# Stick-breaking attention block on one core: the later modulation moved behind attention, the convolution off GpSimd, more split weights in stock

## The chip, the cores and the metric

The kernel runs on one core of one Trainium2 chip. The metric is the device time of one execution in microseconds (us); a kernel's time is the median of its runs. In the profile PE is TensorE's matmuls, PEld its weight loads, DVE is VectorE, ACT is ScalarE, POOL is GpSimd and SP is SyncE, whose queue issues most loads. "Lnnn" is a line of the kernel file.

## The reference

One layer (DEPTH = 1) on a sequence of 1024 tokens of width 1024, all in float32:

```python
mod = c_act @ ada_w[l] + ada_b[l]                  # c_act = silu(c)
sh1, sc1, g1, sh2, sc2, g2 = split(mod, 6)         # sections 0 to 5
h = rmsnorm(x, ln1_g[l]) * (1.0 + sc1) + sh1
p = h @ w_in[l]                                    # 1024 x 8192
q, k, v, cb, cc, cx, ga, gb = split(p)             # eight times 1024
q, k = rmsnorm of q and k per head (16 heads of 64)
y_a = stick_breaking_attention(q, k, v)
y_b = cb * causal_dwconv(cc * cx, conv_w[l])       # three taps per channel
merged = sigmoid(ga) * (y_a @ w_branch_a[l]) + sigmoid(gb) * (y_b @ w_branch_b[l])
x = x + g1 * (merged @ w_out[l])
h = rmsnorm(x, ln2_g[l]) * (1.0 + sc2) + sh2
f = (silu(h @ w_ffn_gate[l]) * (h @ w_ffn_up[l])) @ w_ffn_down[l]
x = x + g2 * f
```

For a query t and a key s < t, stick-breaking attention weighs v[s] by sigmoid(z[t,s]) times the product of 1 - sigmoid(z[t,j]) over the keys j between s and t, with z = q.k / 8.

## The kernel before, in words

Every large product is made of three fast matmuls: each operand is split into a high and a low part in a rounded 32-bit format (`whi` and `wlo` for a weight), and high x high, high x low and low x high are added up in PSUM. A split is a copy on ACT (the high part) and a subtraction on DVE (the low part). So a weight that has been loaded can be used by PE only after ACT and then DVE have had it.

The work goes through these stages:

- **Start** (to about 60 us): the norm of x, and sections 0 and 1 of the modulation.
- **Keys and half of the values** (to about 190 us).
- **Gate stage** (about 190 to 620 us): the loop over `gates` makes, in this order, the queries (section 5 of the list, four steps), the two inputs of the convolution (sections 1 and 2 alternating, eight steps) and the two sigmoid gates (sections 4 and 3, eight steps). Each step is a product of a 1024 x 256 block of weights with all of h by Strassen's scheme: seven products (`g_prod`) of twelve matmuls instead of eight. Its sums of weights (`ws`) are made on POOL; weights and sums are split by `g_split`, whose buffers `whi` and `wlo` are `GS` = 4 deep. The results are put together on DVE (`c`). `put_q` squares a query tile on POOL and splits the square for the sums that the norm needs (L540). `put_u` multiplies the two inputs of the convolution on POOL and makes the three taps: one on POOL, one on ACT, a sum on POOL, the last one on DVE.
- In the gate stage runs also the generator `mods_later`: it makes the later sections 2 to 5 of the modulation. For each section eight tiles of 128 x 1024 (`mada`, two buffers) are loaded from ACT's queue and summed into `macc` with the entries of c as factors (L492, L494 on DVE); then small matmuls with ones sum over the partitions (L253 for columns, L507 for the rows that are broadcast). Three steps of it are taken per gate step from the fifth on. Sections 2 and 5 (g1 and g2) go to DRAM (`d_g`), sections 3 and 4 stay in `mod`.
- **Attention** (about 625 to 1080 us): per head and block of 128 queries scores on PE, two sigmoids on ACT, a scan (L710) and a product (L712) on DVE, transposes, a split and the product with v. Between them, as fillers, run the other values, the product of `cb` with the convolution, whose split result (`ybh`, `ybl`, the low part on POOL, L829) goes to DRAM and comes back, and the branch-b product.
- **Branch-a product** (about 1090 to 1185 us): the loop `for m in range(KT)` loads a weight (`load_ch`), makes two groups of 24 matmuls in two PSUM banks, multiplies with the gate, adds branch b (L933, L934) and splits. `preload_wo` loads and splits the first three output weights in a pool `wpx` that lies where the attention's pool was.
- **Output product with the second norm** (to about 1275 us), **gate and up of the FFN** (to about 1700 us), **down** (to the end).

Tiles are allocated in pools that are opened and closed like a stack on two sides of SBUF; a tile in a new pool waits for those that lay there before. The order of instructions on each engine is not the program's: a scheduler places them by a simulated timeline, with the program's order as priority, and the chip then keeps to that order in each engine's queue. DMAs are issued from the queues of SP, ACT and POOL, in order with what else stands there.

Of the kernel before, what the change touches and what calls it, by code (L numbers as in the profile page):

```python
# [8 lines left out]
F32 = mybir.dt.float32  # L9
F32R = mybir.dt.float32r  # L10
AF = mybir.ActivationFunctionType
# [18 lines left out]
def block_kernel(tc, x, x_t, cols, ada_1, ada_2, ada_row, w_q, w_kv, w_v1, w_cg, w_a, w_b, w_o, w_g, w_u, w_d, out):  # L30
# [8 lines left out]
    def nm(s):  # L39
        uid[0] += 1  # L40
        return f"{s}_{uid[0]}"
# [54 lines left out]
    cst = const.tile([P, 82], F32, name="cst")  # L96
    nc.scalar.dma_start(cst, cols)
    ct, ln1, ln2 = cst[:, 0:8], cst[:, 8:16], cst[:, 16:24]
    acol = cst[:, 24:56].rearrange("p (m k) -> p m k", m=4)
    cw = cst[:, 56:80].rearrange("p (k t) -> p k t", k=8)  # L100
    qgc, kgc = cst[:, 80:81], cst[:, 81:82]
    nc.vector.tensor_scalar(out=qgc, in0=qgc, scalar1=0.125, scalar2=None, op0=ALU.mult)
    mod = const.tile([P, 4, 8], F32, name="mod")
    rqs = ExitStack()
# [144 lines left out]
    def mod_cols(m, acc, k0, kn):  # L249

        ps = g_ss()
        for j in range(kn):
            nc.tensor.matmul(ps[:, j:j + 1], acc[:, j * P:(j + 1) * P], ones[:, 0:1], start=True, stop=True)  # L253
        nc.vector.tensor_tensor(out=mod[:, m, k0:k0 + kn], in0=ps[:, :kn], in1=acol[:, m, k0:k0 + kn], op=ALU.add)

    def norm_x(k, n):
        src = xt[:, k, n * 512:(n + 1) * 512]
# [174 lines left out]

    last_raw = [None]

    def g_split(src):
        hi = gw.tile([P, 512], F32R, tag="whi", bufs=GS, name=nm("whi"))
        lo = gw.tile([P, 512], F32R, tag="wlo", bufs=GS, name=nm("wlo"))
        nc.scalar.activation(hi, src, AF.Copy)  # L438
        tt(nc.vector, lo, src, hi.bitcast(F32), ALU.subtract)
        return hi, lo  # L440
# [35 lines left out]
    gp = sg_.enter_context(tc.tile_pool(name="phg1", bufs=1, reuse_waits="tile"))  # L476

    ft[6] = gp.tile([P, 2, 4, 512], F32R, name="ft6")
    for q, t in ft.items():
        fac[q] = (t[:, 0], t[:, 1])  # L480
    fac[3] = (hh[1][:, 0:4], hl[1][:, 0:4])

    def mods_later():

        for sec in SECS:
            acc = gp.tile([P, D], F32, tag="macc", bufs=1, name=nm("macc"))
            for k in range(8):
                ad = gp.tile([P, D], F32, tag="mada", bufs=2, name=nm("mada"))
                with tc.issue_after(evac[0].ins):
                    nc.scalar.dma_start(ad, ada_2[SECS.index(sec), k])  # L490
                if k == 0:
                    nc.vector.tensor_scalar(out=acc, in0=ad, scalar1=ca[:, k:k + 1], scalar2=None, op0=ALU.mult)  # L492
                else:
                    nc.vector.scalar_tensor_tensor(out=acc, in0=ad, scalar=ca[:, k:k + 1], in1=acc,  # L494
                                                   op0=ALU.mult, op1=ALU.add)
                yield
            yield
            yield
            if sec in (3, 4):
                mod_cols(sec - 1, acc, 0, 8)  # L500
            else:
                e = 0 if sec == 2 else 1
                gb_ = gp.tile([P, D], F32, tag="mada", bufs=2, name=nm("mgb"))
                nc.scalar.dma_start(gb_, ada_row[e:e + 1, :].broadcast_to([P, D]))
                for n in range(2):
                    ps = g_ss()
                    nc.tensor.matmul(ps, ones, acc[:, n * 512:(n + 1) * 512], start=True, stop=True)  # L507
                    nc.vector.tensor_tensor(out=gb_[:, n * 512:(n + 1) * 512], in0=ps,
                                            in1=gb_[:, n * 512:(n + 1) * 512], op=ALU.add)
                nc.scalar.dma_start(d_g[e], gb_)  # L510
            yield

    def g_ss():
        return ps_tr()

    ssq = [g_ss()[:H] for n in range(2)]
    evac = [None]
    ml = mods_later()
# [9 lines left out]
    def put_q(c, m, n):  # L528

        sq = g_tile()  # L530
        tt(nc.gpsimd, sq, c, c, ALU.mult)
        sh, sl, hi, lo = (g_tile(F32R) for _ in range(4))
        nc.scalar.activation(hi, c, AF.Identity, scale=qgc)
        nc.vector.scalar_tensor_tensor(out=lo, in0=c, scalar=qgc, in1=hi.bitcast(F32), op0=ALU.mult, op1=ALU.subtract)
        for e, t in ((0, hi), (1, lo)):
            nc.scalar.dma_start(d_q[e][m, :, n * 512:(n + 1) * 512], t.bitcast(F32))
        nc.scalar.activation(sh, sq, AF.Copy)
        tt(nc.vector, sl, sq, sh.bitcast(F32), ALU.subtract)
        for t in (sh, sl):
            nc.tensor.matmul(ssq[n], sel[:, 14 - 2 * m:30 - 2 * m], t, start=(nss[n] == 0), stop=(nss[n] == 15))  # L540
            nss[n] += 1
# [18 lines left out]
    def put_u(c, m, n):  # L560

        u = uu[m // 4]
        s = n * 512
        tt(nc.gpsimd, u[:, 2 + s:514 + s], c, ccs[m, n], ALU.mult)
        if n == 0:
            uc[m] = True
        elif not uc.get(m):
            raise ValueError(m)
        y, y1 = g_tile(), g_tile()
        nc.gpsimd.tensor_scalar(out=y, in0=u[:, s + 2:s + 514], scalar1=cw[:, m, 2:3], scalar2=None, op0=ALU.mult)  # L570
        nc.scalar.activation(y1, u[:, s + 1:s + 513], AF.Copy, scale=cw[:, m, 1:2])
        tt(nc.gpsimd, y, y, y1, ALU.add)
        nc.vector.scalar_tensor_tensor(out=y, in0=u[:, s:s + 512], scalar=cw[:, m, 0:1], in1=y, op0=ALU.mult, op1=ALU.add)
        nc.scalar.dma_start(d_y[m, :, s:s + 512], y)

# [6 lines left out]
    for g, (sec, j) in enumerate(gates):  # L582
# [31 lines left out]
                with tc.issue_after(ws4.ins):  # L614
                    next(eq, None)

        evac[0] = nc.scalar.activation(c11, p1, AF.Copy)
# [21 lines left out]
        if g + 1 == len(gates):  # L639
            for _ in eq:  # L640
                pass
        for _ in range((0 if sec == 5 else 3) if g + 1 < len(gates) else 50):
            next(ml, None)
    sg_.close()
    gws.close()
    ftx.close()
    gws = ExitStack()
    gw = gws.enter_context(tc.tile_pool(name="wpb", bufs=1, side="right", reuse_waits="tile"))
    for e in range(2):
        nc.sync.dma_start((hh, hl)[e][1][:, :4].bitcast(F32), d_h[e])  # L650
    psA.close()
# [137 lines left out]
    def fillers():  # L789
# [24 lines left out]
        for m, n in [(m, n) for m in range(KT - 2) for n in range(2)] + [(m, n) for n in range(2) for m in (KT - 2, KT - 1)]:  # L814
            if n == 0:
                cb_w[m] = load_ch(w_cg[0, m])
            w = cb_w[m]
            y = fp.tile([P, 512], F32, tag="st", bufs=3, name=nm("cy"))
            nc.sync.dma_start(y, d_y[m, :, n * 512:(n + 1) * 512])
            ps = ps_f()  # L820
            for kk in range(0, KT, KQ):
                if kk:
                    yield 0.65 * KQ
                mm_ch(ps, w, hh[n], hl[n], kk, kk + KQ)
            nc.vector.tensor_tensor(out=y, in0=ps, in1=y, op=ALU.mult)
            yh = fq.tile([P, 512], F32R, tag="ybh", bufs=2, name=nm("ybh"))
            yl = fq.tile([P, 512], F32R, tag="ybl", bufs=2, name=nm("ybl"))
            nc.scalar.activation(yh, y, AF.Copy)  # L828
            nc.gpsimd.tensor_tensor(out=yl, in0=y, in1=yh.bitcast(F32), op=ALU.subtract)  # L829
            nc.scalar.dma_start(d_yb[0][n][:, m, :], yh.bitcast(F32))  # L830
            nc.scalar.dma_start(d_yb[1][n][:, m, :], yl.bitcast(F32))
            yield 0.65 * KQ
# [54 lines left out]
    fqpool.close()  # L887


    swx = ExitStack()  # L890
    wx = swx.enter_context(tc.tile_pool(name="wpx", bufs=1, side="right", reuse_waits="tile"))
    w_pre = []

    def preload_wo():
# [469 lines left out]
```

## Time and profile before

| | |
|---|---|
| median of 3 runs | 1940.23 us (1938.12 to 1941.57) |
| profiled execution | 1936.22 us |
| its span | 1934.4 us |
| granted TensorE clock, mean | 0.986 |
| busy PE / DVE / ACT / POOL | 1850.6 / 1462.6 / 865.2 / 637.7 us |
| moved by DMA | 347.47 MB, mean 180 GB/s |

A row of the instruction groups reads: line, engine, operation, output<-input with shapes, count | busy time in us, mean of one in ns | idle time of the engine before them and who ended it. Matmuls overlap and their ends are modelled, so the distance from start to start tells the pace of PE, and a "busy" PE need not be at its peak. A row of the waits reads: who waited, for whom, us in total, times, longest.

### The profile page before, as it was taken

Reading aid. Unit: us, or ns where it says so; the run is one execution under the profiler, and the core shown is the slowest. Engines: PE = TensorE matmul, PEld = TensorE weight load, DVE = VectorE, ACT = ScalarE, POOL = GpSimd, SP = SyncE. Lnnn points to the kernel's source line nnn. Section 1 sums busy time; section 2 is a strip of 40 time slices with the busy share of each in tenths; the row PEclk is TensorE's granted clock in tenths of the full one; section 3 lists DMA queues with packets and bytes.
Section 4 is the critical chain, followed back from the end, with each engine's and each line's share of the span. In section 5 each row is a group of like instructions: output and inputs, shape, how many; then the busy total and the mean of one; then the engine's idle time right before and its main releaser. Section 6 shows DMA issues by size and latency. Waiting matters only on the chain.

```text
span 1934.4 us, 25157 instructions
## 1 busy us (share of the span) xinstructions
PE 1850.6 (96%) x8869; PEld 1518.1 (78%) x8869; DVE 1462.6 (76%) x1960; ACT 865.2 (45%) x1597; POOL 637.7 (33%) x453
## 2 busy tenths in 40 slices
PE   7899999998999899999999999979999999999999
PEld 4678767777888888887888788867888888888787
DVE  8865787788664799998999644389988788843855
ACT  4532343223333677776777421373444434422221
POOL 3693647977231001111000000055445445301013
PEclk8999999999999999999999999999999999999999
DMA  6555544334445666668654535423444434389666
GB/s 277 178 189 173 201 158 158 131 114 159 161 171 201 207 168 182 169 175 286 178 161 132 190 124 190 139 87 115 158 158 169 153 140 164 133 310 336 246 222 224
DMA packets 151149, 347.47 MB, mean 180 GB/s; under 512 B 15088, under 2 KB 52208, under 8 KB 149104
## 3 DMA queue, kind: packets, MB, share of 16 engines
q1 hardware_dynamic: 74000, 218.80, 34.3%
q10 hardware_dynamic: 76016, 123.40, 17.7%
q0 software_dynamic: 1008, 3.67, 0.5%
q8 instruction: 70, 1.15, 0.2%
q14 instruction: 55, 0.45, 0.1%
HBM read 235.19 MB, written 110.62 MB: 179 GB/s over the span
## 4 chain that ended last, share of the span: by engine, by line
PE 44%; DVE 10%; DMA 3%; issue 2%; ACT 2%; POOL 0%; SPq 0%; ACTq 0%; DVEq 0%
PE e L122 6%; PE e L123 6%; PE e L124 6%; PE e L1203 3%; PE e L1204 3%; PE e L1202 3%; PE pj L785 3%; PE pj L786 3%; PE pj L787 3%; DVE pt L710 2%; PE tr L726 1%; DVE wlo L965 1%; PE e L1020 1%; PE e L1022 1%; PE e L1021 1%
## 5 line engine op out<-in xcount | busy, mean ns | idle before, releaser
L710 DVE TENSOR_TENSOR_SCAN pt<-pt,dm 128x256 f32<-128x256 f32 (+7 forms) x128 | 174.0, 1363 | 4.7 <-ACT pt L705 4.6
L123 PE MATMUL e<-big,whi 128*128 128x512 f32 x352 | 138.4, 393 | 7.6 <-DVE big L127 7.5
L122 PE MATMUL e<-big,whi 128*128 128x512 f32 x352 | 138.0, 392 | 0.8 <-ACT c L1118 0.8
L124 PE MATMUL e<-big,wlo 128*128 128x512 f32 x352 | 137.9, 392 | 0.0
L124 PE MATMUL pj<-big,wlo 128*128 128x512 f32 x320 | 127.5, 399 | 6.6 <-DVE wlo L127 6.6
L276 PE MATMUL pj<-whi,big 128*128 128x512 f32 x352 | 116.8, 412 | 15.0 <-ACT big L263 10.3
L122 PE MATMUL pj<-big,whi 128*128 128x512 f32 x320 | 128.1, 400 | 0.2 <-ACT whi L438 0.2
L1203 PE MATMUL e<-wlo,f 128*128 128x512 f32 (+1 forms) x319 | 122.9, 385 | 4.7 <-DVE wlo L965 4.7
L123 PE MATMUL pj<-big,whi 128*128 128x512 f32 x320 | 127.1, 397 | 0.0
L705 ACT ACTIVATE pt<-z,rq 128x512 f32<-128x512 f32 (+2 forms) x192 | 112.5, 588 | 30.4 <-PE z L704 17.3
L1204 PE MATMUL e<-whi,f 128*128 128x512 f32 (+1 forms) x319 | 122.2, 384 | 0.0
L113 POOL TENSOR_SCALAR rs_m<-ss 128x1 f32<-128x1 f32 x8 | 1.5, 192 | 361.9 <-ACT xn L1035 361.9
L127 DVE TENSOR_TENSOR c<-e,c 128x512 f32<-128x512 f32 x154 | 102.9, 682 | 21.0 <-PE e L124 21.0
L1202 PE MATMUL e<-whi,f 128*128 128x512 f32 (+1 forms) x319 | 117.2, 385 | 1.2 <-DVE c L127 1.2
L829 POOL TENSOR_TENSOR ybl<-cy,ybh 128x512 fp32r<-128x512 f32 x16 | 29.0, 1812 | 257.6 <-ACT ybh L828 243.4
L438 ACT ACTIVATE whi<-raw 128x512 fp32r<-128x512 f32 x116 | 72.7, 633 | 91.9 <-PE pj L123 33.5
L706 ACT ACTIVATE sg<-z,rq 128x512 f32<-128x512 f32 (+1 forms) x192 | 112.9, 591 | 1.3 <-DVE mb L851 1.3
L127 DVE TENSOR_TENSOR wlo<-ws,whi 128x512 fp32r<-128x512 f32 x80 | 73.8, 942 | 50.9 <-ACT whi L438 50.9
L127 DVE TENSOR_TENSOR c<-pj,c 128x512 f32<-128x512 f32 x140 | 93.2, 682 | 24.1 <-PE pj L124 24.0
L730 DVE TENSOR_TENSOR atl<-tr,ath 128x512 fp32r<-128x512 f32 (+1 forms) x192 | 100.5, 545 | 9.8 <-ACT ath L729 9.4
L729 ACT ACTIVATE ath<-tr 128x512 fp32r<-128x512 f32 (+1 forms) x192 | 90.4, 498 | 35.8 <-PE tr L726 15.3
L127 POOL TENSOR_TENSOR ws<-raw,raw 128x512 f32<-128x512 f32 x41 | 57.3, 1398 | 144.5 <-DMA raw<-w_cg 96.0
(250 smaller groups left out, 5602.9 us busy)
## 6 DMA issues: line engine op xcount, KB each, us to landing
f<-d_f SPq DMA_DIRECT2D x77, 512.0 KB, 4.3
d_f<-fs ACTq DMA_DIRECT2D x70, 512.0 KB, 2.6
raw<-w_cg SPq DMA_DIRECT2D x40, 512.0 KB, 3.4
mada<-ada ACTq DMA_DIRECT2D x32, 512.0 KB, 4.2
raw<-w_g SPq DMA_DIRECT2D x24, 512.0 KB, 3.2
raw<-w_u SPq DMA_DIRECT2D x23, 512.0 KB, 3.2
d_k<-khl ACTq DMA_DIRECT2D x32, 256.0 KB, 2.2
d_q<-gt ACTq DMA_DIRECT2D x32, 256.0 KB, 2.0
```

Source lines behind the costliest of these rows:

```text
L122: nc.tensor.matmul(ps, wh[:, k, :], fh[:, k, :], start=(k == 0), stop=False)
L123: nc.tensor.matmul(ps, wh[:, k, :], fl[:, k, :], start=False, stop=False)
L124: nc.tensor.matmul(ps, wl[:, k, :], fh[:, k, :], start=False, stop=(k == 3))
L127: eng.tensor_tensor(out=out, in0=a, in1=b, op=op)
L276: nc.tensor.matmul(ps, a, b, start=(k == 0 and q == 0), stop=(k == KT - 1 and q == 2))
L705: nc.scalar.activation(pt[:, off + s0:off + s0 + m], z[:, :m], AF.Sigmoid, scale=rq[:, 1, i, h:h + 1])
L706: nc.scalar.activation(sg[:, s0:s0 + m], z[:, :m], AF.Sigmoid, scale=rq[:, 0, i, h:h + 1])
L710: nc.vector.tensor_tensor_scan(out=pt[:, rev], data0=pt[:, rev], data1=dm[:, rev], initial=0.0, op0=ALU.mult, op1=ALU.add)
L730: nc.vector.tensor_tensor(out=tl[:, :nb, c0:c0 + P], in0=src, in1=th[:, :nb, c0:c0 + P].bitcast(F32), op=ALU.subtract)
L1202: nc.tensor.matmul(o, sh, w[0][:, c], start=(j == 0), stop=False)
L1203: nc.tensor.matmul(o, sh, w[1][:, c], start=False, stop=False)
L1204: nc.tensor.matmul(o, sl, w[0][:, c], start=False, stop=(j == NJ - 1))
```

## The change

It has three parts.

- The later modulation leaves the gate stage. The generator is rebuilt and runs in the branch-a loop, six steps in each of the first six rounds, the rest in the seventh. c is broadcast to all partitions (`cab`) and multiplied with its sigmoid. The weights lie transposed in DRAM, so that one instruction, `tensor_tensor_reduce`, multiplies a tile of 128 x 1024 with `cab` and sums along the row into one column of `ms`. Sections 3 and 4 add their bias and are done. Sections 2 and 5 add theirs and are broadcast by eight small matmuls with the identity each. The tiles `mada` have five buffers, in a new pool `wpm`; `wpx` opens when it is closed. Bias rows for sections 2 and 5 come with the constants, so two broadcast loads of them go.
- In `put_q` the square goes from POOL to ACT. In `put_u` the product u goes from POOL to DVE, the first tap from POOL to ACT, and the second tap and the sum become one multiply-add on DVE. In the fillers `ybl` goes from POOL to DVE.
- `g_split` takes its buffers in turn from two pools, in the gate stage from `gw` and `gp`, so that eight split weights can stand ready.

```diff
+    gcol = cst[:, 82:98].rearrange("p (m k) -> p m k", m=2)
...
+    split_at = [gw]
+
     def g_split(src):
-        hi = gw.tile([P, 512], F32R, tag="whi", bufs=GS, name=nm("whi"))
-        lo = gw.tile([P, 512], F32R, tag="wlo", bufs=GS, name=nm("wlo"))
+        split_at.append(split_at.pop(0))
+        hi = split_at[0].tile([P, 512], F32R, tag="whi", bufs=GS, name=nm("whi"))
+        lo = split_at[0].tile([P, 512], F32R, tag="wlo", bufs=GS, name=nm("wlo"))
...
+    split_at.append(gp)
...
-    def mods_later():
-
-        for sec in SECS:
-            acc = gp.tile([P, D], F32, tag="macc", bufs=1, name=nm("macc"))
-            for k in range(8):
-                ad = gp.tile([P, D], F32, tag="mada", bufs=2, name=nm("mada"))
-                with tc.issue_after(evac[0].ins):
-                    nc.scalar.dma_start(ad, ada_2[SECS.index(sec), k])
-                if k == 0:
-                    nc.vector.tensor_scalar(out=acc, in0=ad, scalar1=ca[:, k:k + 1], scalar2=None, op0=ALU.mult)
-                else:
-                    nc.vector.scalar_tensor_tensor(out=acc, in0=ad, scalar=ca[:, k:k + 1], in1=acc,
-                                                   op0=ALU.mult, op1=ALU.add)
-                yield
...
     def put_q(c, m, n):
 
         sq = g_tile()
-        tt(nc.gpsimd, sq, c, c, ALU.mult)
+        nc.scalar.activation(sq, c, AF.Square)
...
-        tt(nc.gpsimd, u[:, 2 + s:514 + s], c, ccs[m, n], ALU.mult)
+        tt(nc.vector, u[:, 2 + s:514 + s], c, ccs[m, n], ALU.mult)
...
-        y, y1 = g_tile(), g_tile()
-        nc.gpsimd.tensor_scalar(out=y, in0=u[:, s + 2:s + 514], scalar1=cw[:, m, 2:3], scalar2=None, op0=ALU.mult)
-        nc.scalar.activation(y1, u[:, s + 1:s + 513], AF.Copy, scale=cw[:, m, 1:2])
-        tt(nc.gpsimd, y, y, y1, ALU.add)
+        y = g_tile()
+        nc.scalar.activation(y, u[:, s + 2:s + 514], AF.Copy, scale=cw[:, m, 2:3])
+        nc.vector.scalar_tensor_tensor(out=y, in0=u[:, s + 1:s + 513], scalar=cw[:, m, 1:2], in1=y, op0=ALU.mult, op1=ALU.add)
...
-        for _ in range((0 if sec == 5 else 3) if g + 1 < len(gates) else 50):
-            next(ml, None)
...
-            nc.gpsimd.tensor_tensor(out=yl, in0=y, in1=yh.bitcast(F32), op=ALU.subtract)
+            nc.vector.tensor_tensor(out=yl, in0=y, in1=yh.bitcast(F32), op=ALU.subtract)
...
-    swx = ExitStack()
-    wx = swx.enter_context(tc.tile_pool(name="wpx", bufs=1, side="right", reuse_waits="tile"))
+    smx = ExitStack()
+    mx = smx.enter_context(tc.tile_pool(name="wpm", bufs=1, side="right", reuse_waits="tile"))
+    cab = mx.tile([P, D], F32, name="cab")
+
+    def mods_later():
+
+        csb = mx.tile([P, D], F32, tag="mada", bufs=5, name=nm("csb"))
+        nc.scalar.dma_start(cab, ada_row[0:1, :].broadcast_to([P, D]))
+        nc.scalar.activation(csb, cab, AF.Sigmoid)
+        tt(nc.vector, cab, cab, csb, ALU.mult)
+        for q, sec in enumerate(SECS):
+            ms = mx.tile([P, 8], F32, tag="msum", bufs=2, name=nm("msum"))
+            for k in range(KT):
+                ad = mx.tile([P, D], F32, tag="mada", bufs=5, name=nm("mada"))
+                nc.scalar.dma_start(ad, ada_2[q, k])
+                nc.vector.tensor_tensor_reduce(out=ad, in0=ad, in1=cab, scale=1.0, scalar=0.0, op0=ALU.mult,
+                                               op1=ALU.add, accum_out=ms[:, k:k + 1])
+                yield
+            if sec in (3, 4):
+                tt(nc.vector, mod[:, sec - 1], ms, acol[:, sec - 1], ALU.add)
+                continue
+            e = 0 if sec == 2 else 1
+            tt(nc.vector, ms, ms, gcol[:, e], ALU.add)
+            gb_ = mx.tile([P, D], F32, tag="mada", bufs=5, name=nm("mgb"))
+            for n in range(2):
+                ps = pps.tile([P, 512], F32, tag="z", bufs=NZ, name=nm("z"))
+                for i in range(4):
+                    nc.tensor.matmul(ps[:, i * P:(i + 1) * P], ms[:, 4 * n + i:4 * n + i + 1].broadcast_to([P, P]), ident,
+                                     start=True, stop=True)
+                nc.scalar.activation(gb_[:, n * 512:(n + 1) * 512], ps, AF.Copy)
+            nc.scalar.dma_start(d_g[e], gb_)
+            yield
...
     for m in range(KT):
+        for _ in range(6 if m < KT - 2 else 0):
+            next(ml, None)
+        if m == KT - 2:
+            for _ in ml:
+                pass
+            smx.close()
+            swx = ExitStack()
+            wx = swx.enter_context(tc.tile_pool(name="wpx", bufs=1, side="right", reuse_waits="tile"))
         if m == KT - 1:
             preload_wo()
```

More of the change, by code (lines that the diff above doesn't have):

```diff
@@ L95, in block_kernel @@
     nc.vector.memset(nhalf, -0.5)
-    cst = const.tile([P, 82], F32, name="cst")
+    cst = const.tile([P, 98], F32, name="cst")
     nc.scalar.dma_start(cst, cols)
@@ L247, in block_kernel @@
     hl = [big() for n in range(2)]
[L249 to L254, printed above, removed]
     def norm_x(k, n):
@@ L481, in block_kernel @@
     fac[3] = (hh[1][:, 0:4], hl[1][:, 0:4])
-    def mods_later():
-        for sec in SECS:
-            acc = gp.tile([P, D], F32, tag="macc", bufs=1, name=nm("macc"))
-            for k in range(8):
-                ad = gp.tile([P, D], F32, tag="mada", bufs=2, name=nm("mada"))
-                with tc.issue_after(evac[0].ins):
-                    nc.scalar.dma_start(ad, ada_2[SECS.index(sec), k])
-                if k == 0:
-                    nc.vector.tensor_scalar(out=acc, in0=ad, scalar1=ca[:, k:k + 1], scalar2=None, op0=ALU.mult)
-                else:
-                    nc.vector.scalar_tensor_tensor(out=acc, in0=ad, scalar=ca[:, k:k + 1], in1=acc,
-                                                   op0=ALU.mult, op1=ALU.add)
-                yield
[L497 to L511, printed above, removed]
     def g_ss():
@@ L516, in block_kernel @@
     ssq = [g_ss()[:H] for n in range(2)]
-    evac = [None]
-    ml = mods_later()
     uu = [gp.tile([P, T + 2], F32, name=f"uu{e}") for e in range(2)]
@@ L615, in later @@
                     next(eq, None)
-        evac[0] = nc.scalar.activation(c11, p1, AF.Copy)
+        nc.scalar.activation(c11, p1, AF.Copy)
         p4 = g_prod(g_split(a22), 3) if g + 1 == len(gates) else None
@@ L648, in block_kernel @@
     gw = gws.enter_context(tc.tile_pool(name="wpb", bufs=1, side="right", reuse_waits="tile"))
+    split_at[:] = [gw]
     for e in range(2):
@@ L887, in block_kernel @@
     fqpool.close()
-    swx = ExitStack()
-    wx = swx.enter_context(tc.tile_pool(name="wpx", bufs=1, side="right", reuse_waits="tile"))
+    smx = ExitStack()
[28 more added lines that the diff above has]
+            yield
+    ml = mods_later()
     w_pre = []
@@ L1335 @@
         np.asarray(conv_w)[0].reshape(3, KT, P).transpose(2, 1, 0).reshape(P, 3 * KT),
-        np.tile(np.asarray(q_norm_g)[0], 2).reshape(P, 1), np.tile(np.asarray(k_norm_g)[0], 2).reshape(P, 1)], axis=1)
+        np.tile(np.asarray(q_norm_g)[0], 2).reshape(P, 1), np.tile(np.asarray(k_norm_g)[0], 2).reshape(P, 1),
+        ab[[2, 5]].reshape(2 * KT, P).T], axis=1)
     arrays = {
@@ L1341 @@
         "ada_1": cc(aw[:, :, :2].transpose(3, 1, 0, 2, 4).reshape(KT, P, KT, 256)),
-        "ada_2": cc(aw[:, :, SECS].transpose(2, 0, 1, 3, 4).reshape(4, KT, P, D)),
-        "ada_row": cc(ab[[2, 5]]),
+        "ada_2": cc(aw[:, :, SECS].transpose(2, 3, 4, 0, 1).reshape(4, KT, P, D)),
+        "ada_row": cc(np.asarray(c)),
         "w_q": tcols(wi[:, :D]),
```

## The prediction

> **What bounds the kernel now.** First the page: the engine shares and the strips.
>
> ```profile
> span 1934.4 us, 25157 instructions
> PE 1850.6 (96%) x8869; PEld 1518.1 (78%) x8869; DVE 1462.6 (76%) x1960; ACT 865.2 (45%) x1597; POOL 637.7 (33%) x453
> ...
> DVE  8865787788664799998999644389988788843855
> POOL 3693647977231001111000000055445445301013
> ```
>
> TensorE is busy 96% of the span, so a gain has to come from gaps in its queue or from matmuls it no longer runs. The two strips show where other engines are full: POOL at 7 to 9 tenths in the seventh to tenth slice (290 to 484 us, in the gate stage), and DVE at 9 nearly throughout the fifteenth to twenty-second (677 to 1064 us, attention). The profiled execution took 1936.22 us with 1934.4 us of span, 0.2% under the median of the runs, 1940.23; I work out a difference and take it off the median.
>
> Next the stages by windows. The columns are the window, its length, the busy time of PE, PEld, DVE, ACT and POOL (with the number of instructions), the granted clock, the DMA share and GB/s.
>
> ```profile
> 190.00:290.00 100.00, 95.30 (x411) 72.06 (x410) 75.11 (x94) 40.24 (x67) 52.38 (x38) 1.00 0.52 184
> 290.00:480.00 190.00, 180.63 (x778) 141.90 (x776) 151.21 (x169) 55.62 (x93) 160.19 (x101) 1.00 0.40 139
> 480.00:625.00 145.00, 144.92 (x642) 117.86 (x643) 85.24 (x118) 52.61 (x88) 34.09 (x28) 0.98 0.49 176
> 625.00:1070.00 445.00, 425.38 (x2623) 370.22 (x2623) 411.99 (x590) 329.85 (x708) 28.99 (x16) 0.99 0.62 183
> 1070.00:1090.00 20.00, 17.18 (x86) 14.25 (x85) 15.69 (x24) 9.82 (x19) 0.00 (x0) 0.91 0.67 220
> 1090.00:1156.00 66.00, 66.00 (x284) 53.02 (x283) 33.09 (x50) 16.51 (x27) 0.00 (x0) 1.00 0.46 157
> 1156.00:1185.00 29.00, 29.00 (x126) 23.27 (x126) 10.89 (x16) 4.21 (x7) 0.00 (x0) 1.00 0.37 127
> ```
>
> The gate stage is the first three rows (queries, convolution, gates). In the convolution part POOL is busy 160 of 190 us and PE has 9.4 us of visible gaps. Attention (fourth row) keeps DVE busy 412 of 445 us. The branch-a product, 1090 to 1185, has no PE gap at all, a DVE that is less than half used, and an idle POOL. The change takes work from the first place and puts it into the last. What PE waits for in the gate stage, and the longest such wait with the matmuls behind it:
>
> ```profile
> PE pj L124 <- DVE wlo L127: 6.6, 4, 3.8
> PE pj L122 <- ACT whi L438: 4.4, 5, 1.5
> PE tr L540 <- DVE gt L127: 1.8, 3, 0.7
> PE tr L540 <- ACT gt L537: 1.1, 2, 0.6
> ...
> 475.68 0.39 PE L122 MATMUL pj<-big,whi 128*128 128x512 f32 x1
> 475.92 0.40 PE L123 MATMUL pj<-big,whi 128*128 128x512 f32 x1
> 480.08 0.79 PE L124 MATMUL pj<-big,wlo 128*128 128x512 f32 x1 [3.77 <-DVE wlo L127]
> 480.67 0.63 PE L122 MATMUL pj<-big,whi 128*128 128x512 f32 x1
> ...
> 485.36 0.49 PE L124 MATMUL pj<-ft,wlo 128*128 128x512 f32 x1
> ```
>
> All are waits for a split weight or a split square, 13.9 us together. The long one also lowers the clock: from 480.67 to 485.36 eleven matmuls take 4.69 us, where their spacing before the wait (0.23 to 0.24 us) would give 2.6.
>
> **Why the splits come late.** The same microseconds on DVE and POOL, then groups of the whole gate stage:
>
> ```profile
> 473.12 2.31 DVE L494 SCALAR_TENSOR_TENSOR macc<-mada,ca,macc 128x1024 f32<-128x1024 f32 x1
> ...
> 474.30 2.28 POOL L127 TENSOR_TENSOR ws<-raw 128x512 f32<-128x512 f32 x1
> ...
> L494 DVE SCALAR_TENSOR_TENSOR macc<-mada,ca,macc 128x1024 f32<-128x1024 f32 x28 | 41.1, 1468 | 12.5 <-DMA mada<-ada 12.4
> ...
> L492 DVE TENSOR_SCALAR macc<-mada,ca 128x1024 f32<-128x1024 f32 x4 | 3.3, 837 | 2.2 <-DMA mada<-ada 2.2
> ...
> L573 DVE SCALAR_TENSOR_TENSOR gt<-uu,cst,gt 128x512 f32<-128x512 f32 x16 | 23.0, 1440 | 14.6 <-POOL gt L127 14.6
> ...
> L507 PE MATMUL tr<-macc,ones 128*128 128x512 f32 x8 | 3.8, 591 | 0.0
> ...
> L253 PE MATMUL tr<-ones,macc 128*128 128x1 f32 x32 | 3.7, 245 | 0.0
> ...
> L494 DVE SCALAR_TENSOR_TENSOR macc<-mada,ca,macc x28: 1271/1284/2319, 295.9 to 568.2; 128x1024 f32<-128x1024 f32 x28
> ```
>
> A modulation sum (L494) takes 1.27 us at its fastest and 2.31 us here, while POOL's subtraction, begun during it, takes 2.28: each lengthens the other. Right behind the sum on DVE stand the evacuations and the `wlo` for which PE is waiting.
>
> **The change, part by part.**
>
> *Gate stage, PE.* The sums of the later modulation leave, and with them their matmuls (L507, L253): 3.8 + 3.7 = 7.5 us of PE time gone. Of the waits I take away those of the convolution part, among the contended instructions: 190 - 180.6 = 9.4 us by its window; the 4.7 us of the first window I leave but for 1 us (the square in front of L540 goes from POOL to ACT). The gap of 3.77 us in the list is 4.16 from start to start against 0.24, so each wait hides about 0.15 more: 1.2 for some eight (nine in the first two rows of the waits, less one at the front of the stage). The clock dip gives 4.69 - 2.6 = 2.1. Sum: 7.5 + 9.4 + 1 + 1.2 + 2.1 = **21.2 us off**. If the waits had another cause, only the 7.5 would go.
>
> *Gate stage, what takes the work.* DVE loses L494 and L492 (44.4 us) and gains, 16 times each, a product u and a multiply-add of the kind of L573; even at that row's contended 1.44 us for both kinds these are 46 us, and without POOL beside them about half. So DVE does not get fuller. ACT gains 16 squares of a 128x512 tile, under 12 us beside 40.2 busy of 100: nothing, unless PE waits for ACT there, and then at most those 12. Eight split weights instead of four let ACT and DVE split one step further ahead; this costs no instruction, only room which the sums leave. The 32 loads and two broadcasts of a bias row leave ACT's queue.
>
> *Attention.* The subtraction for `ybl` goes from POOL to DVE, which is nearly full there:
>
> ```profile
> L127 DVE TENSOR_TENSOR wlo<-raw,whi 128x512 fp32r<-128x512 f32 x37 | 24.9, 674 | 0.0
> ...
> 715.00:910.00 195.00, 46.19 (x56) 1.00 0.66 198
> 910.00:1060.00 150.00, 33.54 (x46) 0.99 0.57 166
> ```
>
> On DVE it costs 16 x 0.674 = 10.8 us. Against it stands the end of the contention. The last two rows are DVE's product with the scan (L712) in the heads that run beside `ybl` and in those after: 0.825 and 0.729 us each, 5.5 us over 57 of them, and the scans lose some more in the same way. Between -1 (the scans as much as that again, and a shorter way to the last reload) and +5.3, I take **+2**.
>
> *Behind attention, DVE.* 32 fused multiply-and-sums of 128x1024 come in. No such instruction is in the trace. The nearest rows are L494 alone (1.27 us, two fp32 inputs from SBUF, no sum along the row), ACT's read of an accumulator, and the scan, which carries a value from element to element:
>
> ```profile
> L1035 ACT ACTIVATION_READ_ACCUMULATOR xn<-x x8: 182/184/187, 1232.8 to 1280.3; 128x1 f32 x8
> ...
> L710 DVE TENSOR_TENSOR_SCAN pt<-pt,dm 128x1024 f32<-128x1024 f32 x15 | 34.2, 2280 | 0.6 <-ACT pt L705 0.6
> ```
>
> That brackets one at 1.27 to 2.28 + 0.18 = 2.46. I take 1.27 + 0.18 = 1.45, near L494, because a plain sum is one more addition per element behind the product: 32 x 1.45 and 2 for the rest (c times its sigmoid, four small additions) are 48 us. DVE's idle time from 1070 to 1185 is 4.3 + 32.9 + 18.1 = 55.3 us. They fit, but only if they run to about 1170. So two things become late. DVE's evacuations of the branch-a product stand behind a sum or two, and PE has two banks to run ahead; and the second pool `wpx`, which now opens only when the sums are done, loads the first output weights some 100 us later, in SP's queue ahead of the last branch-a loads. I put **+6 us** of PE waiting on both (0 to 26, the upper end from the price of 2.46).
>
> *Behind attention, PE.* 16 small fp32 matmuls replace the ones above. In the start stage 8 of the same kind (L242) are 16 records, so these are 32; a run of eight 128-wide records takes 1.04 us below: **+4.2**, half of that if each is one record.
>
> ```profile
> L242 PE MATMUL tr<-dm,rs_r x16: 421/421/582, 18.2 to 23.3; 128*128 128x128 f32 x16
> ...
> 1241.55 1.04 PE L983 MATMUL e<-dm,xn 128*128 128x128 f32 x8
> ```
>
> They stand in PE's order behind the sums: if a sum is later than planned, all matmuls after them wait.
>
> Sum: -21.2 + 2 + 6 + 4.2 = **-9.0 us**: 1927.2 for the profiled execution, **1931** for the median.
>
> **The rivals.** A difference of 0.2% (4 us) is about what a measurement of this kernel can tell from none.
>
> *Slower: the fused sum runs at half rate.* At 2.46 us the 32 take 78.7 + 2 = 80.7 us, 25.4 more than DVE's idle time, and the branch-a product waits for DVE. Then -21.2 + 2 + 4.2 + 25.4 = +10.4: **1950**. It decides where that excess reaches 15.0, at 70.3 us or (70.3 - 2) / 32 = 2.13 us each. Against it stands L494, which streams two fp32 operands at 1.27; for it the scan's 2.28. [...] Chance 0.18.
>
> *No change: the loads come late.* Rows of the loads as they are, and the fullest stretches of the trace:
>
> ```profile
> mada<-ada ACTq DMA_DIRECT2D x32, 512.0 KB, 4.2
> ...
>   ACT whi L438: 15.1, 5
> ...
> 10.00:20.00 10.00, 7.72 (x32) 4.52 (x30) 9.21 (x19) 4.74 (x9) 3.11 (x3) 0.90 1.03 429
> 610.00:620.00 10.00, 10.00 (x47) 8.19 (x46) 5.40 (x9) 3.26 (x7) 0.19 (x4) 1.00 1.00 372
> 1075.00:1156.00 81.00, 78.27 (x338) 63.26 (x339) 43.78 (x68) 24.96 (x42) 0.00 (x0) 0.98 0.51 173
> ```
>
> 32 loads and the broadcast of c, 33 x 0.524 MB, on top of 81 us at 173 GB/s would be 387 GB/s to be done by 1156, between the 372 and 429 at which the queues were full. ACT waited 15.1 us for the sums in the gate stage, because a load in its queue waited for a buffer; behind such a load now stand the splits of `w_a`. If those 15 us reach PE in place of the 6, the sum is 0.0: **1940**. For it: the full queues. Against: five buffers instead of two, no contention, and half the stage's work needed late. Chance 0.16.
>
> *Slower a little: the gate stage's waits stay* (ACT and DVE late for their new work) and only 7.5 us go there: -7.5 + 12.2 = +4.7, **1945**. The idle shares of DVE and ACT speak against it. Chance 0.11.
>
> **How the numbers follow.** The forecast has 0.55: 1931, within it 1920 (all 13.9 us of waits gone, nothing lost behind attention) to 1936. With the others the range is **1920 to 1952**, which leaves out a price of the sum above 2.46 us or a second wait on top. Faster 0.55; same 0.16; slower 0.29.
>
> **What would show it.** Right: no PE wait over 2 us between 290 and 480, L127 `wlo` near 0.69 us throughout the gate stage, this stage 20 us shorter; the fused sum near 1.45 us; PE's gaps from 1070 to the output product under 10 us together. Wrong: a fused sum over 2 us, PE waiting for DVE's evacuations or for the sums' matmuls, the first output weights landing after the branch-a product ends, or gate-stage waits that remain with POOL idle.

## The result and the profile after

The changed kernel takes 1943.23 us (median of 14 runs) against 1939.76 (14 runs of the kernel before on the same chip): a ratio of 1.0029, 95% interval 1.0017 to 1.0041. By the ratio it is slower by 0.3%, some 5.6 us (the two medians differ by 3.5), where 9 us less were forecast. The profiled execution has a span of 1938.7 us against 1934.4.

The page of the kernel after, engine shares and strips:

```profile
span 1938.7 us, 25136 instructions
PE 1850.9 (95%) x8861; PEld 1522.6 (79%) x8861; DVE 1461.6 (75%) x2039; ACT 877.1 (45%) x1618; POOL 510.1 (26%) x373
...
DVE  8865677877453999998999774489988888844854
POOL 3694327432320000000000000055445344301014
...
DMA  6465542222328555677564965422444434389666
```

POOL has 128 us less to do, DVE as much as before, PE as much as before. The work was moved, and the time with it. In the strip of the DMA share (tenths) the middle of the gate stage is down to 2 and the slice behind attention, the twenty-third, is up to 9.

The same stages by windows, with the bounds shifted to where the stages now lie (columns: window, length, busy PE, PEld, DVE, ACT, POOL, granted clock, DMA share, GB/s):

```profile
290.00:480.00 190.00, 187.64 (x812) 150.47 (x811) 144.29 (x188) 63.08 (x104) 88.00 (x56) 1.00 0.25 88
480.00:605.00 125.00, 125.00 (x549) 101.31 (x548) 61.15 (x87) 44.65 (x74) 28.18 (x24) 1.00 0.35 122
605.00:1050.00 445.00, 426.21 (x2634) 372.41 (x2633) 411.57 (x602) 328.06 (x704) 0.00 (x0) 0.99 0.63 184
1050.00:1076.00 26.00, 19.59 (x101) 16.60 (x100) 22.52 (x37) 8.76 (x18) 0.00 (x0) 0.87 0.85 298
1076.00:1142.00 66.00, 58.98 (x237) 45.46 (x236) 53.16 (x94) 15.41 (x26) 0.00 (x0) 0.92 0.92 340
1142.00:1183.00 41.00, 40.47 (x182) 32.58 (x180) 20.64 (x33) 9.79 (x17) 0.00 (x0) 1.00 0.33 118
```

In the convolution part PE's gaps are down from 9.4 to 2.4 us, the tail of the waits for the queries' squares; from 302 to 605 us PE has none. The branch-a product, which had none, now has 7.0 us of gaps in 66, at a granted clock of 0.92 and a DMA share of 0.92 (0.46 before).

Distances in us between the same matmuls in both traces say it more exactly, for one profiled execution each. The gate stage is counted from the first matmul with a Strassen factor to the first of the other values; attention from the first score to the first branch-a matmul on y_a (so it holds the seam); the branch-a product from its first to its last matmul on y_a; the rest of the way to the FFN's first matmul on `rh` holds the output product.

| | before | after | difference |
|---|---|---|---|
| gate stage | 413.2 | 395.6 | -17.6 |
| attention and seam | 459.2 | 462.4 | +3.2 |
| branch-a product | 89.4 | 105.9 | +16.5 |
| output product, second norm | 131.8 | 132.6 | +0.8 |

With 1.4 us elsewhere this is the 4.3 us of the spans. The gate stage gave most of the 21.2 that were forecast; the branch-a product took nearly all of it back, and attention the rest. Who PE waited for, in the gate stage and behind attention (190 to 605 and 1045 to 1192 us):

```profile
PE tr L506 <- DVE gt L128: 4.0, 3, 2.3
PE pj L123 <- ACT whi L435: 2.3, 1, 2.3
PE tr L506 <- ACT gt L503: 2.1, 4, 0.7
...
PE tr L690 <- DVE atl L694: 4.3, 2, 2.5
PE pj L749 <- DVE sgi L937: 4.0, 3, 3.1
PE pj L749 <- ACT ya L914: 2.8, 1, 2.8
```

L506 was L540: the waits for the squares of the queries have doubled. L749 is the branch-a product, L937 its evacuation and L914 the split of y_a. The new instruction (durations in ns, min/median/max) and the loads (last column: median us from issue to landing):

```profile
L869 DVE CUSTOM_DVE_ANT_0 mada<-mada,cab x32: 1202/1220/1227, 1062.9 to 1141.9; 128x1024 f32<-128x1024 f32 x32
...
1064.07 0.08 DVE L869 DVE_READ_ACCUMULATOR2_ANT msum<- 128x1 f32 x1
...
mada<-ada ACTq DMA_DIRECT2D x32, 512.0 KB, 6.2
...
yr<-d_ya SPq DMA_DIRECT2D x16, 256.0 KB, 4.5
...
raw<-w_a SPq DMA_DIRECT2D x8, 512.0 KB, 6.0
```

And the last two loads in the kernel before:

```profile
yr<-d_ya SPq DMA_DIRECT2D x16, 256.0 KB, 3.0
...
raw<-w_a SPq DMA_DIRECT2D x8, 512.0 KB, 4.0
```

The fused sum is cheap, 1.22 us and 0.08 for the read of its result. What has become dear are the loads: `yr`, which brings y_a back, lands after 4.5 us instead of 3.0, and `w_a` after 6.0 instead of 4.0.

### The profile page after: what moved, and what is told of

It reads as the page before. It is cut to its first block, busy times and chain, and to the rows that moved or that the text cites. A ratio compares the mean times of both kernels' runs of the same rounds, so it can differ in the third digit from the quotient of the medians.

```text
span 1938.7 us, 25136 instructions
## 1 busy us (share of the span) xinstructions
PE 1850.9 (95%) x8861; PEld 1522.6 (79%) x8861; DVE 1461.6 (75%) x2039; ACT 877.1 (45%) x1618; POOL 510.1 (26%) x373
## 3 DMA queue, kind: packets, MB, share of 16 engines
q10 hardware_dynamic: 75872, 122.89, 17.3%
## 4 chain that ended last, share of the span: by engine, by line
PE 65%; DVE 15%; DMA 8%; ACT 4%; issue 4%; POOL 3%; ACTq 0%; SPq 0%; DVEq 0%; POOLq 0%
PE e L124 7%; PE e L125 7%; PE e L123 7%; PE pj L124 5%; PE pj L123 5%; PE pj L125 5%; PE e L1207 3%; PE e L1208 3%; PE e L1206 3%; PE pj L749 3%; DVE pt L674 3%; PE pj L750 3%; PE pj L751 3%; DVE acc L205 2%; PE pj L270 2%
## 5 line engine op out<-in xcount | busy, mean ns | idle before, releaser
L674 DVE TENSOR_TENSOR_SCAN pt<-pt,dm 128x256 f32<-128x256 f32 (+7 forms) x128 | 171.4, 1342 | 10.4 <-ACT pt L669 10.2
L128 DVE TENSOR_TENSOR wlo<-raw,whi 128x512 fp32r<-128x512 f32 x116 | 92.2, 799 | 27.7 <-ACT whi L435 27.7
L124 PE MATMUL e<-rl,whi 128*128 128x512 f32 x264 | 103.5, 392 | 1.8 <-DVE rl L128 1.8
L690 PE MATMUL tr<-dm,sg 128*128 128x128 f32 x576 | 93.1, 277 | 12.3 <-DVE atl L694 11.3
```

Source lines behind the costliest of these rows:

```text
L124: nc.tensor.matmul(ps, wh[:, k, :], fl[:, k, :], start=False, stop=False)
L128: eng.tensor_tensor(out=out, in0=a, in1=b, op=op)
L674: nc.vector.tensor_tensor_scan(out=pt[:, rev], data0=pt[:, rev], data1=dm[:, rev], initial=0.0, op0=ALU.mult, op1=ALU.add)
```

## The experiments

Theory D: the 32 loads fill the DMA queues behind attention, and what the branch-a product needs comes late. Theory V: the fused sums stand before its evacuations in DVE's order. Theory P: in the gate stage POOL's work makes the waits, and the move wasn't needed there.

**Loads or sums.** Three versions of the change. The first:

```diff
+        held = []
+        scr = csb
...
-                ad = mx.tile([P, D], F32, tag="mada", bufs=5, name=nm("mada"))
-                nc.scalar.dma_start(ad, ada_2[q, k])
-                nc.vector.tensor_tensor_reduce(out=ad, in0=ad, in1=cab, ...
+                if len(held) < 3:
+                    ad = mx.tile([P, D], F32, tag="mada", bufs=5, name=nm("mada"))
+                    nc.scalar.dma_start(ad, ada_2[q, k])
+                    held.append(ad)
+                nc.vector.tensor_tensor_reduce(out=scr, in0=held[k % len(held)], in1=cab, ...
```

> The change, but only three of the 32 tiles of the later modulation are loaded behind attention; all 32 fused sums run, on those three tiles again and again (27 of 32 sums and so the later modulation have wrong data). DVE's work is that of the change, 29 x 0.5 MB of DMA are gone. In the change the branch-a product takes 105.9 us from its first to its last matmul, against 89.4 before, with the DMA queues at 0.92. Theory D (the loads fill the queues, and yr, w_a and the sums come late): the product goes back to 89.4 plus 4 for the small matmuls, 92 to 95 us, and the time falls to 0.993 to 0.995 of the kernel before. Theory V (the sums stand in DVE's order before the evacuations): the product stays at 102 to 106 us and the time at 1.002 to 1.004.

The second keeps the loads and takes `ad[:, :8]` and `cab[:, :8]` in the sum:

> The change with all 32 loads, but each fused sum takes 8 columns instead of 1024 (so the later modulation lacks most of its terms). DMA is that of the change, 32 x 1.1 us of DVE are gone. Theory D: the product stays at 100 to 106 us, the time at 1.000 to 1.004. Theory V: the product goes to 92 to 95 us and the time to 0.993 to 0.995. If both have a share, this run and the one with three loads each win a part, and the parts add up to what the run with neither wins.

The third does both:

> The change with three of 32 loads and with sums over 8 columns (the later modulation lacks most of its terms). Both theories: the product near 93 us, so that the change keeps its gate stage (17.7 us less) and attention (2.7 us less) and pays only the small matmuls (4): 0.991 to 0.993 of the kernel before. If it stays above 0.998, neither loads nor sums are the cause, but the new order of the end of attention and of the output weights.

| | ratio to before | interval | branch-a product, us |
|---|---|---|---|
| the change | 1.0029 | 1.0017 to 1.0041 | 105.9 |
| three loads, full sums | 0.9979 | 0.9963 to 0.9996 | 96.7 |
| all loads, short sums | 1.0065 | 1.0048 to 1.0082 | 115.0 |
| neither | 0.9961 | 0.9948 to 0.9974 | 92.9 |

With neither, the product pays 3.5 us over the 89.4 of before, about the small matmuls. Full sums alone add 3.8; loads alone add 22.1. With both it is 13.0, less than the loads alone. So the parts do not add up, though the second expectation had supposed that they would. A long sum keeps its buffer and so holds back the next load: with short sums the 32 loads are issued within 62 us, in the change within 74. With all loads and short sums, PE's waits from 1045 to 1192 and one window of 25 us:

```profile
PE pj L749 <- ACT ya L914: 10.9, 3, 4.7
PE tr L690 <- DVE atl L694: 4.7, 2, 3.0
PE pj L749 <- DVE sgi L937: 2.0, 1, 2.0
...
1100.00:1125.00 25.00, 18.23 (x59) 12.75 (x58) 10.34 (x49) 4.93 (x8) 0.00 (x0) 0.80 1.00 380
```

DVE is busy 10 of 25 us, the DMA share is 1.00, PE waits for the split of y_a, and the clock falls to 0.80. So the loads do most of the harm (theory D), the sums 3.8 us (theory V). Both runs with three loads were slower than expected (0.993 to 0.995 and 0.991 to 0.993). In the third the branch-a product is as expected, in the first it is 1.7 us over its 95. In their profiles attention and seam take 467.6 and 464.5 us, against 459.2 before, where the expectation of the third run had counted on 2.7 us less; why they do is open.

**The other half of the change alone.** The kernel before with convolution, square and `ybl` off POOL, as in the diff of the change; sums in the gate stage, four split weights:

> The kernel before with the second part of the change alone: convolution, square and ybl off GpSimd; the later modulation stays in the gate stage, four split weights in stock. By the prediction's step the waits in the convolution part came from POOL and the sums together: with POOL's part gone 8 to 12 of the 12.7 us of waits and clock dip go, 0.994 to 0.996. If the sums alone are the cause, or the stock of four, under 4 us go: 0.998 to 1.000.

0.9890 (0.9871 to 0.9909): 21 us faster than before, more than the expectation gave it. PE's waits in its gate stage (190 to 605), and the window in which POOL had been full:

```profile
PE pj L122 <- ACT whi L438: 3.4, 1, 3.4
PE tr L540 <- ACT gt L537: 0.6, 1, 0.6
...
300.00:480.00 180.00, 180.00 (x783) 145.35 (x782) 150.72 (x203) 56.56 (x93) 83.67 (x53) 1.00 0.44 151
```

Not one wait is left in the convolution part, with the sums still there. The gate stage takes 396.2 us, 17.0 less than before, the branch-a product 89.5. (The span of the profile is 13.1 us shorter than before; where the rest of the 21 lies it does not show.)

**The fused sums in the gate stage.** The same, with the new generator of the change in the old place:

```diff
-    cab = mx.tile([P, D], F32, name="cab")
+    cab = gp.tile([P, D], F32, name="cab")
...
-                ad = mx.tile([P, D], F32, tag="mada", bufs=5, name=nm("mada"))
-                nc.scalar.dma_start(ad, ada_2[q, k])
+                ad = gp.tile([P, D], F32, tag="mada", bufs=3, name=nm("mada"))
+                with tc.issue_after(evac[0].ins):
+                    nc.scalar.dma_start(ad, ada_2[q, k])
```

> The second part of the change, with the later modulation by the fused sums of the change (1.22 us each), but in the gate stage where it was, three buffers, four split weights in stock. Theory D (behind attention the loads fill the queues; in the gate stage, with POOL relieved, there is room for them): the gate stage as in the run without the move (396 us from the first matmul with a Strassen factor to the first of the other values, 413 before) less some 3 us for fewer small matmuls, the branch-a product at 89 to 90 us, and 0.986 to 0.989 of the kernel before. Rival (the sums do not belong in the gate stage, whatever POOL does): waits for split weights come back there, 0.992 or more.

0.9875 (0.9854 to 0.9895), 1915.46 us: the fastest version, some 24 us below the kernel before and 28 below the change (its interval overlaps that of the run without the move). Gate stage 394.0, branch-a product 89.4.

**POOL's work back, with the move and the eight split weights kept:**

> The change with convolution, square and ybl back on GpSimd; the move and the eight split weights stay. Theory P (POOL's work in the gate stage and its contention with DVE make the waits, and the sums only add to them): the gate stage stays at 405 to 413 us, and with the branch-a product at 105 the time is 1.008 to 1.014. Rival (the sums in DVE's order make the waits, as the prediction also allowed): the gate stage falls to 396 to 400 us and the time is that of the change, 1.001 to 1.005.

1.0048 (1.0029 to 1.0067), gate stage 404.9: the stage at the edge of theory P, the time in the range of its rival. The waits that are left are not those of before:

```profile
PE tr L506 <- DVE gt L128: 7.8, 6, 2.6
PE tr L506 <- ACT gt L503: 2.4, 4, 1.3
PE pj L123 <- ACT whi L435: 2.2, 1, 2.2
```

They lie in the queries. There is none in the convolution part, though POOL is nearly as loaded there as before (150 of the 180 us from 300 to 480, against 160). So the stock came under suspicion.

**Four split weights in the change**, one line:

```diff
-    split_at.append(gp)
```

> The change with four split weights in stock, as before. If the stock does nothing once POOL is relieved: gate stage 395 to 397 us, time 1.001 to 1.005, as the change. If the stock carries a part of the gain: gate stage over 399 us, time 1.005 or more. If it does harm in the query part, where the change waits 6.1 us for the squares' splits and the run without the move 0.6: gate stage under 393 us, time under 1.001.

0.9987 (0.9974 to 1.0000), gate stage 388.2 us against 395.6, and the row of the squares' matmuls:

```profile
L505 PE MATMUL tr<-gt,sel 128*16 128x512 f32 x32 | 12.6, 394 | 0.9 <-ACT gt L502 0.9
```

**Eight only behind the queries:**

```diff
-    split_at.append(gp)
...
     for g, (sec, j) in enumerate(gates):
+        if g == 4:
+            split_at.append(gp)
```

> The change with eight split weights only from the fifth gate step on, that is behind the queries; four before. If the larger stock harms the query part alone (splits of later weights in front of the squares' splits): query part, from the first Strassen matmul to the last square's matmul, 86 to 88 us as with four (94.8 in the change), gate stage 387 to 390 us, time 0.997 to 1.000. If it harms anywhere: gate stage over 392 us.

0.9997 (0.9986 to 1.0008), gate stage 389.0: as expected; the query part, 88.5, is half a us over. The larger stock costs the gate stage about 7 us, in the query part alone, and brings nothing behind it (300.8 us with eight, 301.6 with four). How it does so was not tested apart. In the profiles of both runs with four in the queries attention and seam take 468.5 us, 6 more than in the change, which is not explained.

**The move alone**, on the kernel before with four split weights:

> The kernel before with the move alone: the later modulation behind attention by fused sums; convolution, square and ybl on GpSimd, four split weights. Theory (each of the two, sums away or POOL's work away, ends the waits of the convolution part by itself; the loads cost 17 us behind attention): gate stage 395 to 400 us against 413 before and 388 with both, branch-a product 103 to 108, time 1.001 to 1.005. If POOL's work makes the waits alone: gate stage 405 or more and time over 1.007.

1.0028 (1.0014 to 1.0042), gate stage 394.9, branch-a product 109.0. PE's waits in its gate stage:

```profile
PE pj L123 <- ACT whi L435: 2.1, 2, 1.7
PE tr L505 <- DVE gt L128: 1.6, 3, 0.7
PE tr L505 <- ACT gt L502: 1.1, 2, 0.6
PE pj L125 <- DVE wlo L128: 0.3, 1, 0.3
```

Here POOL is almost as full as before (155 of 180 us), and all but 0.6 us of the waits of the convolution part are gone all the same. With the sums gone or with POOL's work gone: either ends them, so they need both. Theory P is true only in that the move wasn't needed.

**The loads alone.** The fastest version with the 32 loads of the change behind attention, read by nothing:

```diff
+    def idle_loads():
+        for q in range(4):
+            for k in range(KT):
+                ad = mx.tile([P, D], F32, tag="mada", bufs=5, name=nm("mada"))
+                nc.scalar.dma_start(ad, ada_2[q, k])
+                yield
```

> The version with the fused sums in the gate stage, and in addition the 32 loads of the change behind attention into the same five buffers, which nothing reads; no sums and no small matmuls there. Theory D: the loads alone lengthen the branch-a product from 89.4 to 100 to 115 us, and the time is 0.993 to 1.001 against 0.9875 without them. If it was the sums in DVE's order, or ACT waiting for buffers behind sums: the product under 95 us and the time under 0.991.

1.0025 (1.0009 to 1.0042), branch-a product 111.7 us: 22 us more than without them, and 1.5% of the time. PE's waits from 1045 to 1192, and the load of y_a:

```profile
PE pj L783 <- ACT ya L926: 11.6, 3, 5.3
PE o L739 <- DVE oy L744: 4.0, 2, 3.7
...
yr<-d_ya SPq DMA_DIRECT2D x16, 256.0 KB, 5.8
```

No sum, no small matmul and no wait for a sum's buffer is left to blame. (`wpx` opens late here too; the stretch that holds the output product is 132.6 against 131.8.)

The loads do harm in two ways, though, and this run does not part them. From the chain of work that ended last (start, us, what; a DMA from issue to landing), first in this run, then in the change:

```profile
1089.40 8.79 DMA mada<-ada
1098.22 9.55 DMA mada<-ada
1107.80 0.33 ACTq L896
1108.17 0.64 ACT ya L926
...
1079.08 6.36 DMA yr<-d_ya
1085.46 0.64 ACT ya L914
...
1086.84 8.07 DMA yr<-d_ya
1094.93 0.64 ACT ya L914
```

Here ACT can issue a load only when an earlier one has landed and freed its buffer (five are there), and the split of y_a stands behind it in ACT's order. From 1045 to 1192 the moved loads are 27.4% of the chain and `yr` 5.7%; in the run with all loads and short sums it is 12.8% and 9.1%. In the change `yr` is 17.3%, and no moved load is in the chain: there what is shown is the late landing.

**Two buffers in the change**, `bufs=2` for `mada`:

> The change with two buffers for the moved loads instead of five, so that at most two of them are under way. Theory D: the loads are spread, yr lands in under 4 us instead of 4.5, PE's waits in the branch-a product shrink, 98 to 103 us instead of 105.9, and the time is 0.997 to 1.001. If instead ACT's queue is what hurts (splits behind a load that waits for its buffer): more such waits, the product over 108 us, 1.005 or more.

1.0020 (1.0008 to 1.0032), branch-a product 103.1, `yr` 3.8 us. The product is at the edge of what D expected and the time is above it: the last of the loads is issued at 1169.5 us instead of 1132.5, `wpx` opens only behind it, and the stretch of the output product takes 136.1 us against 132.6. Now the sums wait for their loads, 17.4 us in all.

**`ybl` back on POOL**, in the fastest version:

> The version with the fused sums in the gate stage, with ybl back on GpSimd. By the prediction's step (ybl on DVE costs 10.8 us of DVE there and saves about 9 of contention) attention with its tail, from the first score to the first branch-a matmul on y_a, stays within 3 us of the 460 us it takes with ybl on DVE, and the time at 0.986 to 0.989. If the contention weighs more: 463 us or over and 0.989 to 0.992; if DVE's fullness does: under 457 us and below 0.986.

0.9900 (0.9887 to 0.9913), just over the expected 0.986 to 0.989, attention and seam 460.8 us against 460.4. The intervals overlap: no difference that can be told.

## Why the prediction was wrong

*The waits of the convolution part: right in size, wrong in what it took.* Behind the queries the gate stage went from 321.4 us to 300.8, -20.5; 7.5 + 9.4 + 1.2 + 2.1 = 20.2 were forecast for it. But the prediction took one edit and the other as one cause. The runs with only the sums gone and with only POOL's work gone show that each ends the waits, so once POOL is relieved the move wins little: 396.2 - 388.2 = 8.0 us of gate stage at a stock of four. That this is near the 7.5 of the small matmuls is partly luck: 5.3 of it lie behind the queries, where these ran, and 2.7 in the query part, where none did. Nor did the splits get fast. `wlo` was to be near 0.69 us throughout the stage; the rows of before, then of the change, from 190 to 606:

```profile
L127 DVE TENSOR_TENSOR wlo<-ws,whi 128x512 fp32r<-128x512 f32 x79 | 73.1, 945 | 48.7 <-ACT whi L438 48.7
L127 DVE TENSOR_TENSOR wlo<-raw,whi 128x512 fp32r<-128x512 f32 x56 | 47.7, 852 | 0.0
...
L128 DVE TENSOR_TENSOR wlo<-ws,whi 128x512 fp32r<-128x512 f32 x80 | 61.3, 769 | 32.9 <-ACT whi L435 30.5 <-DMA d_k<-khl 2.2
L128 DVE TENSOR_TENSOR wlo<-raw,whi 128x512 fp32r<-128x512 f32 x60 | 54.6, 913 | 23.2 <-ACT whi L435 23.2
```

At means of 0.77 and 0.91 us PE waits for none of them.

*The stock of eight: costed at nothing, the first step that failed.* "This costs no instruction, only room" was true and not the question. In the change PE waits 6.1 us for the squares, where 2.9 before and 1 us less were forecast; with four in stock it waits 0.9, and the gate stage is 7.4 us shorter.

*Attention: +2 forecast, +3.2 measured.* The +2 was for `ybl`, which costs nothing that can be told (460.4 us on DVE, 460.8 on POOL). The three profiles with the modulation left in the gate stage and nothing loaded behind attention have 460 to 461 us, those with the move 462 to 469. The loads alone give 463.9, but the move with only three loads is no shorter (467.6 and 464.5); on single profiles the cause of the 3.2 stays open.

*The fused sum: 1.45 us taken, 1.22 + 0.08 measured.* The 32 of the change take 1.20 to 1.23 us each, so the rival at half rate, priced at 2.46, does not hold. Of the 0.15 us under the forecast 0.05 lie in the sum itself (1.22 against L494's 1.27) and 0.10 in the read of its result, which was taken from ACT's row at 0.18 and took 0.08 on DVE. Why the sum along the row adds nothing to the 1.23 us that a plain product of this shape takes in the change (`cab` with its sigmoid) no run shows.

*The branch-a product: the second step that failed.* +6 for late evacuations and late output weights and +4.2 for the small matmuls, 10.2, stand against 16.5 + 0.8 measured. The matmuls are nearly right (3.5, in the run with neither loads nor sums). The 6 was worked out from DVE's idle time, which did suffice: sums without loads add 3.8. What is missing in it is the loads, which the sum put at nothing: loads and sums together add 13.0 to the product (105.9 - 92.9) where 6 stood, and 9.2 of these go when 29 of the 32 loads are left out. They stood in the rival "the loads come late", with 387 GB/s worked out from the rows and 1940 us as its time, and this is the case that came, 3 us worse. Its chance of 0.16 was too low: a demand between the two fullest stretches of the trace is no margin. By the same rows the moved and the old bytes, 17.3 + 14.0 MB, would fill the queues for 73 to 84 us at 429 to 372 GB/s, an estimate; the stage has 81. The detail of that rival, splits on ACT behind a load that waits for its buffer, is met in the run with the loads alone, where an earlier load holds the buffer; in the change one split of a weight stands so for 4.7 us, behind a load that waits for a sum, but not in the chain that ended last.

The errors add up: 4 us in the queries, 7 in the branch-a product, 1 in attention and 1 elsewhere make the 13 between -9.0 and +4.3.

Not settled: how much of the change's loss is `yr` and how much the other late loads, the evacuations behind the sums and the lower clock after the waits. PE's waits there are shared between the split of y_a (2.8 us) and the evacuations (4.0).

## What to carry to other kernels

Before moving loads beside a stage that PE fills, add their bytes to that stage's own and hold the rate against the fullest stretches of the trace; here, at a DMA share of 0.92 where it had been 0.46, the loads that the stage needs landed late (`yr` after 4.5 us instead of 3.0, `w_a` after 6.0 instead of 4.0), though DVE's idle time had room for the sums; and in the run with the loads alone ACT, which issues them, stood behind a load of 9.55 us whose buffer it needed, with the split of y_a behind it. When two edits relieve the same wait, price each alone: here the one that left the modulation in place was worth 21 us, and the two it was shipped with gave them all back. A deeper stock of buffers is not free either; here it cost 7 us, in a way that was not tested.

## What the runs showed of the hardware

- Loads without any consumer, 32 x 0.5 MB, lengthen a product that PE had filled from 89.4 to 111.7 us; `yr` lands after 5.8 us instead of the 3.0 of the kernel before. In the slice of 48.5 us from 1068 on the DMA share is 9 tenths, at 385 GB/s. Part of the lengthening is that ACT, which issues them, stands at loads whose buffer is not yet free: in the chain the issue at 1107.80 follows a load of 9.55 us, and the split of y_a, at 1108.17, follows the issue.
- PE's gaps cost more than their length in these traces. In the kernel before, behind the wait of 3.77 us that ends at 480.08, the granted clock is 0.50 until 485.40 and 0.99 in the ten us after that. In the run with all loads and short sums a 25 us window with waits of 1.8 and 4.4 us, just behind one of 4.7, has a granted clock of 0.80. In the change, behind the wait of 2.8 us that ends at 1095.6, matmuls start 0.4 to 0.7 us apart until 1099.5, at a granted clock of 0.60, and from 1099.9 on 0.23, at 0.99.
- A fused product and sum of 128x1024 in float32 takes 1.22 us, no more than the plain multiply-add with its 1.27 at the fastest, and 0.08 for the read of the accumulator; in the gate stage, beside POOL's remaining work, its mean is the same:

```profile
L492 DVE CUSTOM_DVE_ANT_0 mada<-mada,cab 128x1024 f32<-128x1024 f32 x32 | 39.0, 1222 | 22.7 <-DMA mada<-ada 22.7
```
